# Another order for the branches' steps and their weights, and the norm rows loaded while the branches are merged

## The chip, the cores and the metric

The kernel runs as one program on one core of a Trainium2 chip. The time of a kernel is the device time of one execution in microseconds (us). Engines: PE is TensorE (matmuls and transposes; PEld its weight loads), DVE is VectorE, ACT is ScalarE, POOL is GpSimd, SP is SyncE, which here only issues transfers. Each engine works off its own instructions in the order in which the program holds them, and waits on semaphores of the others.

## The reference, cut to what matters

A block of two layers is followed by a second block of two layers, on a sequence of 512 tokens of width 1024. Each layer of the first block runs four attention branches of four heads, gates each with a silu, merges them and ends in a layer norm:

```
h = x @ w_in                         # split into the inputs of all branches
y_mla = causal softmax attention on rms-normed latents c_q, c_kv (w_qb, w_kvb), with rope
y_sb  = stick-breaking attention: a = exp(z + suffix sums of log_sigmoid(-z)), causal
y_fox = causal softmax attention, logits + (c_t - c_s), c = cumsum(log_sigmoid(fox_f + bias))
y_mem = softmax attention on keys and values made of mem (256 rows)
for n, y in enumerate((y_mla, y_sb, y_fox, y_mem)):
    merged += sigmoid(merge_r @ w_merge_up)[n] * ((y * silu(gate_z[n])) @ w_branch[n])
x = layer_norm(ALPHA * x + merged @ w_out, ln_g, ln_b)
```

Each layer of the second block runs four other branches of four heads (a dense, b a window with a sink, c a neighbourhood, d a difference of two softmaxes), gated with silu too, `x = x + mix @ w_out`, and the last row is normed. All is float32.

## The kernel before, in words

All tokens of a layer are on the chip at once. A product in float32 precision is made of three matmuls on split halves (`mm3`, L328 to L330): the two factors are split into a rounded high part (on ACT, L319) and the rest (on DVE, L322). A projection by one 128x1024 weight unit is so 24 matmuls of 128x512 (`proj`, from `proj_fm`). The halves of x stand in `zth`, `ztl`.

A layer of the first block is woven of generators, one for each branch, that yield after each step. `ORDER1` is a string of words that says which generator makes its next step: `first` (two memory queries and one stick query), `g` (a gate: one `proj` unit copied to `z`; after the gates of certain branches one more step runs their silus on ACT), `sb` (7 steps: keys, values, two heads, queries and keys, two heads), `mem` (5: keys and values, four heads), `fox` (8: row sums, queries and keys, values, two heads, queries and keys, two heads), `mla` (12: five latents, their norm, values and the rope queries, keys and queries, two heads, keys and queries, two heads), `misc`, and `f`, which takes the oldest ended pair of heads, divides it by its sums and multiplies it into its gate. `ORDER2` does the same for the second block (a, b, c, d, g, f, and w for a first part of the output product). `WEIGHTS1` and `WEIGHTS2` give the order in which the weight units come in, each by one transfer of 512 KB on SP and a split on ACT and DVE; `w_get` keeps three units ahead (`WP`).

The strings give the order of the program; a scheduler then places each instruction in its engine's own sequence, so that steps lie between each other. A head's chain is: scores on PE into one of three PSUM banks (`s`), a maximum on DVE (L525, L528), exp on ACT (L534), transposes on PE (`T`, L551), their split on ACT and DVE (`th`, `tl`), and the product with the values on PE (`O`, L557, L558). A stick head (`stick_head`) does four blocks: scores, then abs, exp and ln on ACT (L881 to L883) and max on DVE (L884), sums on PE (L894), exp on ACT (L896), the product on PE (`Os`, L900, L901). Silu and sigmoid need another function table on ACT than exp and ln; each change is an ACT_TABLE_LOAD.

After the heads the gated branches `z` are split (`split_z`), `merge` multiplies them by `w_branch` (`projwb`) and their merge gates (`projmu`), and `w_out` and `post` end the layer in four pieces of 128 tokens: product (`pso`), residual (L1127), layer norm (`ln_rows`), transposes back into `zth` and `ztl`. `end` loads the norm's rows `lng` and `lnb` (L1173), and `w_out` the residual rows (L1119), into a pool that is opened when the merge's pool is closed.

Of the kernel before, what the change touches and what calls it, by code (L numbers as in the profile page):

```python
# [18 lines left out]
S = 512  # L19
# [44 lines left out]


WEIGHTS1 = """
mq:0 mq:1 sb:0 gz:6 sb:256 sbv:0 sbv:1 sbv:2 gz:7 gz:2 gz:3 m:0 m:1 mk:0 mk:1 mv:0 mv:1 sb:128 sb:384 fox:0
fox:256 cq:0 cq:1 cq:2 gz:4 gz:5 ckv:0 ckv:1 foxv:0 foxv:1 gz:0 gz:1 fox:128 fox:384 kvb qr qb mr mu:0 wb:0
wb:1 mu:1 wb:2 wb:3 mu:2 wb:4 wb:5 mu:3 wb:6 wb:7 wo:0 wo:1 wo:2 wo:3 wo:4 wo:5 wo:6 wo:7
"""  # L70
WEIGHTS2 = """
qa:0 qa:1 ka qd:0 qd:1 kd qc:0 vd g2:6 g2:7 g2:0 g2:1 vab:0 vab:1 g2:2 g2:3 qb2:0 g2:4 qb2:1 kc:0 kb g2:5 vc:0
qc:1 kc:1 vc:1 we:0 we:1 wo2:0 wo2:1 wo2:2 wo2:3 wo2:4 wo2:5
"""

# [216 lines left out]

ORDER1 = "first g sb2 g misc sb g2 mem4 fox sb3 mem fox g mla f mla g3 mla2 fox mla f2 fox sb g f fox g fox mla fox mla fox mla g f mla f mla f mla2 f"
ORDER2 = "a d3 c d g2 d g2 d a d g f g2 a b a2 f g b c b a b2 g c f c g c d f2 c b f c b c f2 w2"
# [14 lines left out]
class Build:  # L311
# [275 lines left out]

    def new_o(self, r=None):
        return self.op.tile([128, S], F32, tag="o", name="o")

    def gate(self, key, at):

# [311 lines left out]
    def mla(self, l):  # L904
# [31 lines left out]
        qsc = self.kp.tile([128, 4, 2], F32, tag="qsc", name="qsc")  # L936
        nc.vector.tensor_scalar(qsc[:, :, 0], rs[:, :, 0], 96.0**-0.5, None, ALU.mult)
        nc.vector.tensor_scalar(qsc[:, :, 1], rs[:, :, 0], -(96.0**-0.5), None, ALU.mult)
        d = self.tmp("diag").rearrange("p (a b) -> p a b", b=128)
        nc.vector.tensor_copy(d, rs[:, :, 1:2].to_broadcast([128, 4, 128]))  # L940
        rep = self.pst.tile([128, S], F32, tag="T", name="rep")
        for tt in range(4):
            nc.tensor.transpose(rep[:, cols(tt)], d[:, tt], self.ident)
        for c in craw:
            h, lo = self.st("ckh"), self.st("ckl")
            nc.vector.tensor_tensor(c, c, rep, ALU.mult)
# [162 lines left out]
    def w_out(self, kind, l, lhs, post, last):  # L1109
        nc = self.nc  # L1110
        ks = range(len(lhs[0]))
        for k in ks:
            self.w_get((kind, l, k))
        woh, wol = self.wout
        for tt in range(4):
            c = cols(tt)
            y = self.bp.tile([128, DM], F32, tag="y", name="y", bufs=2)
            if kind == "wo":
                nc.sync.dma_start(y, self.resid[c])  # L1119
            fs = [cols(0, 512), cols(1, 512)]  # L1120
            if last and tt == 3:
                fs[1:] = [cols(2, 256), cols(3, 256)]
            for f in fs:
                ps = self.pss.tile([128, S], F32, tag="S", name="pso")[:, : f.stop - f.start]
                self.mm3(ps, [(lhs[0][k][:, c], lhs[1][k][:, c], woh[:, k, f], wol[:, k, f]) for k in ks])
                if kind == "wo":
                    nc.vector.scalar_tensor_tensor(y[:, f], y[:, f], ALPHA, ps, ALU.mult, ALU.add)  # L1127
                else:
                    nc.vector.tensor_tensor(y[:, f], self.early[tt][f.start // 512][:, f.start % 512 :][:, : f.stop - f.start], ps, ALU.add)
            post(tt, y, fs)  # L1130
# [25 lines left out]
    def ln_rows(self, y, g, b):  # L1156
        nc = self.nc
        st, mv, v = self.small(12, "bn"), self.small(2, "mv"), self.small(1, "var")
        for hf in range(2):
            nc.vector.bn_stats(st[:, cols(hf, 6)], y[:, cols(hf, 512)])  # L1160
        nc.vector.bn_aggr(mv, st.rearrange("p (a b) -> p a b", b=6))
        nc.vector.tensor_scalar(v, mv[:, 1:2], LN_EPS, None, ALU.add)
        for hf in range(2):
            f = cols(hf, 512)
            nc.vector.scalar_tensor_tensor(y[:, f], y[:, f], mv[:, 0:1], g[:, f], ALU.subtract, ALU.mult)
        rs = self.rsqrt(v)
        for hf in range(2):
            f = cols(hf, 512)
            nc.vector.scalar_tensor_tensor(y[:, f], y[:, f], rs, b[:, f], ALU.mult, ALU.add)

    def row(self, i, name):
        t = self.bp.tile([128, DM], F32, tag=name, name=name, bufs=1)
# [3 lines left out]
    def run(self):  # L1176
        nc, tc = self.nc, self.tc
        self.setup()
        for L in self.layers:
            l, kind = L % 2, "wo" if L < 2 else "wo2"  # L1180
            last = L == self.layers[-1]
            self.resid = self.ins["x"] if L == self.layers[0] else self.xs[L - 1]
            left = (self.layer1 if L < 2 else self.layer2)(l)
            nk = 8 if L < 2 else 6
            with tc.tile_pool(name=f"b{L}", bufs=1, side="right") as wop, left:
                self.wout = [wop.tile([128, nk, 1024], F32R, tag=f"wo{i}", name="wout") for i in range(2)]
                if L < 2:
                    left.close()
                    with tc.tile_pool(name=f"m{L}", bufs=3, side="left") as mp:
                        self.y = {n: self.split_z(n, mp) for n in MERGE}  # L1190
                        self.merge(l, mp)
                    lhs = [[t[:, k] for k in range(8)] for t in (self.zth, self.ztl)]
                else:
# [6 lines left out]
    def end(self, L, kind, lhs, last):  # L1200

        nc, l = self.nc, L % 2
        if L < 2:
            g, b = self.row(2 * l, "lng"), self.row(2 * l + 1, "lnb")
        gn = self.row(6 if L == 3 else 3 + L, "rmsg") if L == 3 or L in (1, 2) and not last else None

        def post(tt, y, fs):
            c = cols(tt)
            if L < 2:
                self.ln_rows(y, g, b)  # L1210
            if not last:
                nc.sync.dma_start(self.xs[L][c], y)
            if gn is not None:
# [260 lines left out]
```

## Time and profile before

| | us |
|---|---|
| median of 3 runs (1413.12 to 1415.84) | 1414.28 |
| the profiled execution's own time | 1410.68 |
| its span, from the first to the last instruction | 1408.9 |
| PE busy | 1350.6 |
| DVE busy | 1002.5 |
| ACT busy | 828.6 |

The span is that of the core's instructions; the execution's time has 1.8 us more around it. The page's busy time of PE counts matmuls that overlap each other, so 96% is the share of time in which PE had some matmul, not that of its peak. The first projections of the four layers start at 6, 415, 819 and 1112 us. In the rows, a wait is put down to the instruction that released it.

### The profile page before, as it was taken

Reading aid. Unit: us, or ns where it says so; the run is one execution under the profiler, and the core shown is the slowest. Engines: PE = TensorE matmul, PEld = TensorE weight load, DVE = VectorE, ACT = ScalarE, POOL = GpSimd, SP = SyncE. Lnnn points to the kernel's source line nnn. Section 1 sums busy time; section 2 is a strip of 40 time slices with the busy share of each in tenths; the row PEclk is TensorE's granted clock in tenths of the full one; section 3 lists DMA queues with packets and bytes.
Section 4 is the critical chain, followed back from the end, with each engine's and each line's share of the span. In section 5 each row is a group of like instructions: output and inputs, shape, how many; then the busy total and the mean of one; then the engine's idle time right before and its main releaser. Section 6 shows DMA issues by size and latency. Waiting matters only on the chain.

```text
span 1408.9 us, 19990 instructions
## 1 busy us (share of the span) xinstructions
PE 1350.6 (96%) x7096; PEld 1103.6 (78%) x7096; DVE 1002.5 (71%) x2077; ACT 828.6 (59%) x1672; POOL 4.3 (0%) x12
## 2 busy tenths in 40 slices
PE   8999998999999999998999999999999999999897
PEld 7887786777789777876777788877777888878776
DVE  5666545898773777257989775888787576877785
ACT  4585547765413775376856243775865446667663
POOL 0000000000000000000000000000000000000000
PEclk9999999899999999999999999999999999999999
DMA  7543323213625434222125536413535365215241
GB/s 231 166 128 92 90 77 80 61 52 103 232 105 127 142 90 130 75 74 72 48 90 171 182 109 178 122 61 82 143 93 155 117 174 155 62 55 152 66 135 73
DMA packets 61266, 160.31 MB, mean 114 GB/s; under 512 B 11056, under 2 KB 11696, under 8 KB 61168
## 3 DMA queue, kind: packets, MB, share of 16 engines
q1 hardware_dynamic: 61168, 159.05, 38.3%
q8 instruction: 56, 0.92, 0.3%
q14 instruction: 42, 0.34, 0.1%
HBM read 117.92 MB, written 8.91 MB: 90 GB/s over the span
## 4 chain that ended last, share of the span: by engine, by line
PE 75%; DVE 10%; ACT 8%; DMA 4%; issue 2%; SPq 0%; DVEq 0%; ACTq 0%
PE proj L328 11%; PE proj L329 11%; PE proj L330 10%; PE T L551 4%; PE pso L328 3%; PE pso L330 3%; PE pso L329 3%; PE O L557 3%; DMA raw<-in_w_dram 2%; PE O L558 2%; PE projwb L329 2%; PE projwb L328 2%; PE projwb L330 2%; PE projv L329 2%; PE projv L330 2%; PE projv L328 2%
## 5 line engine op out<-in xcount | busy, mean ns | idle before, releaser
L328 PE MATMUL proj<-zth,wh 128*128 128x512 f32 (+1 forms) x864 | 321.7, 373 | 8.3 <-ACT wh L319 5.6
L329 PE MATMUL proj<-ztl,wh 128*128 128x512 f32 (+1 forms) x864 | 322.4, 373 | 0.2
L330 PE MATMUL proj<-zth,wl 128*128 128x512 f32 (+1 forms) x864 | 321.0, 372 | 0.0
L322 DVE TENSOR_TENSOR wl<-raw,wh 128x1024 fp32r<-128x1024 f32 (+2 forms) x153 | 182.8, 1195 | 127.5 <-ACT wh L319 124.5
L319 ACT CAST wh<-raw 128x1024 fp32r<-128x1024 f32 (+2 forms) x153 | 157.5, 1029 | 149.0 <-PE proj L329 112.6
L328 PEld LDWEIGHTS proj<-zth,wh 128*128 128x128 f32 x864 | 164.0, 190 | 33.1 <-ACT wh L319 5.6
L330 PEld LDWEIGHTS proj<-zth,wl 128*128 128x128 f32 x864 | 164.0, 190 | 24.8 <-DVE wl L322 1.0
L329 PEld LDWEIGHTS proj<-ztl,wh 128*128 128x128 f32 x864 | 164.0, 190 | 24.1 <-DVE ztl L322 0.7
L322 DVE TENSOR_TENSOR tl<-T,th 128x512 fp32r<-128x512 f32 (+3 forms) x176 | 99.5, 576 | 36.7 <-ACT th L319 35.6
L319 ACT CAST th<-T 128x512 fp32r<-128x512 f32 (+3 forms) x176 | 85.1, 498 | 55.9 <-PE T L551 53.0
L551 PE MATMUL T<-ct,p 128*128 128x128 f32 x560 | 89.0, 279 | 5.2 <-ACT p L534 4.0
L528 DVE TENSOR_REDUCE nm<-s 128x1 f32<-128x512 f32 (+1 forms) x128 | 77.5, 614 | 14.8 <-PE s L1388 7.6
L551 PEld LDWEIGHTS T<-ct,p 128*128 128x128 f32 x560 | 67.8, 142 | 23.1 <-ACT p L534 7.0
L557 PE MATMUL O<-tl,V 128*128 128x512 f32 (+3 forms) x160 | 62.2, 390 | 8.3 <-DVE tl L322 7.4
L534 ACT ACTIVATE p<-s,nm 128x512 f32<-128x512 f32 (+1 forms) x96 | 59.1, 619 | 16.3 <-DVE nm L528 15.9
L558 PE MATMUL O<-th,V 128*128 128x512 f32 (+3 forms) x160 | 56.5, 355 | 0.0
L328 PE MATMUL pso<-wout,zth 128*128 128x512 f32 x128 | 51.1, 399 | 4.7 <-DVE y L1127 4.7
L329 PE MATMUL projv<-wl,zth 128*128 128x256 f32 (+1 forms) x192 | 54.9, 286 | 0.0
L328 PE MATMUL projv<-wh,zth 128*128 128x256 f32 (+1 forms) x192 | 54.6, 284 | 0.0
L330 PE MATMUL projv<-wh,ztl 128*128 128x256 f32 (+1 forms) x192 | 54.4, 283 | 0.0
L328 PE MATMUL projwb<-y,wh 128*128 128x512 f32 x128 | 51.5, 402 | 0.2
L330 PE MATMUL projwb<-y,wl 128*128 128x512 f32 x128 | 51.5, 403 | 0.0
(380 smaller groups left out, 2904.6 us busy)
## 6 DMA issues: line engine op xcount, KB each, us to landing
raw<-in_w_dram SPq DMA_DIRECT2D x173, 512.0 KB, 4.3
xs<-y SPq DMA_DIRECT2D x12, 512.0 KB
ks<-hs SPq DMA_DIRECT2D x32, 128.0 KB, 2.3
early<-xs SPq DMA_DIRECT2D x16, 256.0 KB, 3.8
bias<-in_bias_dram SPq DMA_DIRECT2D x8, 448.0 KB, 4.0
qs<-hs SPq DMA_DIRECT2D x24, 128.0 KB, 3.4
qs<-ls SPq DMA_DIRECT2D x24, 128.0 KB, 2.3
hs<-ls SPq DMA_DIRECT2D x24, 128.0 KB, 2.6
```

The lines of the kernel that those rows point to most:

```text
L319: self.nc.scalar.copy(h, src)
L322: self.nc.vector.tensor_tensor(l, src, h, ALU.subtract)
L328: self.nc.tensor.matmul(ps, ah, bh, start=i == 0, stop=False)
L329: self.nc.tensor.matmul(ps, ah, bl, start=False, stop=False)
L330: self.nc.tensor.matmul(ps, al, bh, start=False, stop=i == n - 1)
L528: nc.vector.tensor_reduce(nm, s, AX.X, ALU.max, negate=True)
L534: nc.scalar.activation(p[:, :w], src, AF.Exp, bias=nm, scale=sc, accum_out=sm)
L551: nc.tensor.transpose(T[:, cols(a)], P[i][:, c : c + 128], self.ident)
L557: nc.tensor.matmul(o, vsel(j), tl[:, :w], start=j == 0, stop=False, skip_group_check=True)
L558: nc.tensor.matmul(o, vsel(j), th[:, :w], start=False, stop=j == nk - 1, skip_group_check=True)
```

## The change

Four things are edited.

- The order of the steps, in `ORDER1` and `ORDER2`, and that of the weight units with it. The numbers of steps are the same. In the first block the latents (`mla`) begin before the last two stick heads, the last stick head comes ahead of the first forget-gate head instead of behind it, and the last gate unit (`gz:1`) comes behind the projections of the second forget-gate pair instead of ahead of them, with its silu behind that. In the second block steps of a, d and the gates change places.
- The norm rows and the residual rows of the first two pieces are loaded by `load_rows`, eight transfers of 256 KB into the eight buffers of the gates' pool `z`, each of which comes free when its gate has been split; the call stands between the split and the merge.
- The residual of pieces 0 and 1 is read from there (`rows`), and `ln_rows` takes the two halves of each norm row.
- In `mla` the copy `diag` falls away: four transposes read a broadcast of `rs` instead.

```diff
-ORDER1 = "first g sb2 g misc sb g2 mem4 fox sb3 mem fox g mla f mla g3 mla2 fox mla f2 fox sb g f fox g fox mla fox mla fox mla g f mla f mla f mla2 f"
+ORDER1 = "first sb g sb g misc sb g2 mem3 fox mem sb2 fox mem mla2 sb g2 mla g mla f fox mla f2 sb fox2 g2 fox g mla f fox mla g fox mla f2 mla f mla3 f"
...
+    def load_rows(self, l):
+        def load(src):
+            ts = [self.zp.tile([128, S], F32, tag="z", name="row") for _ in range(2)]
+            for hf, t in enumerate(ts):
+                self.nc.sync.dma_start(t, src(cols(hf, 512)))
+            return ts
+
+        self.resid_rows = {0: load(lambda f: self.resid[cols(0), f])}
+        self.lng, self.lnb = (load(lambda f: self.ins["rows"][2 * l + i, f].partition_broadcast(128)) for i in range(2))
+        self.resid_rows[1] = load(lambda f: self.resid[cols(1), f])
...
-        d = self.tmp("diag").rearrange("p (a b) -> p a b", b=128)
-        nc.vector.tensor_copy(d, rs[:, :, 1:2].to_broadcast([128, 4, 128]))
...
-            nc.tensor.transpose(rep[:, cols(tt)], d[:, tt], self.ident)
+            nc.tensor.transpose(rep[:, cols(tt)], rs[:, tt, 1:2].to_broadcast([128, 128]), self.ident)
...
+            rows = self.resid_rows.get(tt) or [y[:, f] for f in (cols(0, 512), cols(1, 512))]
-            if kind == "wo":
+            if kind == "wo" and tt not in self.resid_rows:
                 nc.sync.dma_start(y, self.resid[c])
...
-                    nc.vector.scalar_tensor_tensor(y[:, f], y[:, f], ALPHA, ps, ALU.mult, ALU.add)
+                    nc.vector.scalar_tensor_tensor(y[:, f], rows[f.start // 512], ALPHA, ps, ALU.mult, ALU.add)
...
                         self.y = {n: self.split_z(n, mp) for n in MERGE}
+                        self.load_rows(l)
                         self.merge(l, mp)
...
-            g, b = self.row(2 * l, "lng"), self.row(2 * l + 1, "lnb")
```

Three places show what the scheduler made of it. The first is ACT in layer 0 at the last pair of silus (`z`), before: `zt` and `at` belong to the last stick head, `p` to a forget-gate head.

```order
L601 ACTIVATE z_2260<-z_2260 128x512
L883 ACT_TABLE_LOAD
L883 ACTIVATE zt_2180<-zt_2180 128x256
L601 ACT_TABLE_LOAD
L601 ACTIVATE z_2366<-z_2366 128x512
L896 ACT_TABLE_LOAD
L896 ACTIVATE at_2193<-s_2176 128x256
L881 ACTIVATE zt_2205<-s_2201 128x384
L457 ACTIVATE hs_2430<-proj_2405 128x512
L882 ACTIVATE zt_2205<-zt_2205 128x384
```

One table load stands ahead of these rows and three behind them, up to the one of L604. The same pair after:

```order
L614 ACT_TABLE_LOAD
L614 ACTIVATE z_2330<-z_2330 128x512
L414 CAST V_2489<-projv_2491 128x4x64
L414 CAST V_2489<-projv_2508 128x4x64
L614 ACTIVATE z_2450<-z_2450 128x512
L414 CAST V_2490<-projv_2491 128x4x64
L414 CAST V_2490<-projv_2508 128x4x64
L617 ACT_TABLE_LOAD
```

Seven loads have become two, since nothing of a head lies between the silus: the stick head has ended before. It is the same in layer 1, and no other place has another number of loads.

The second is PE in layer 0 at the fourth forget-gate head, before: its last scores `s_2695`, the product `O_2585` of the head ahead of it, and its first transposes `T_2703`.

```order
L512 MATMUL s_2695<-ks_2482,qs_2434 128x512
L513 MATMUL s_2695<-kr_2478,qr_2435 128x512
L557 MATMUL O_2585<-tl_2602,V_1923 128x384
L558 MATMUL O_2585<-th_2601,V_1923 128x384
L551 MATMUL T_2616<-ct_79,p_2581 128x128
L557 MATMUL O_2585<-tl_2611,V_1923 128x256
L558 MATMUL O_2585<-th_2610,V_1923 128x256
L557 MATMUL O_2585<-tl_2619,V_1923 128x128
L558 MATMUL O_2585<-th_2618,V_1923 128x128
L551 MATMUL T_2703<-ct_79,p_2698 128x128
```

After, `s_2696` are that head's last scores, and `projn` and `s_2749` projections and scores of the next branch:

```order
L512 MATMUL s_2696<-ks_2446,qs_2398 128x512
L513 MATMUL s_2696<-kr_2442,qr_2399 128x512
L328 MATMUL projn_2942<-ckh_2055,wh_2407 128x512
L329 MATMUL projn_2942<-ckl_2056,wh_2407 128x512
L330 MATMUL projn_2942<-ckh_2055,wl_2408 128x512
L328 MATMUL projn_2942<-ckh_2060,wh_2407 128x512
L329 MATMUL projn_2942<-ckl_2061,wh_2407 128x512
L330 MATMUL projn_2942<-ckh_2060,wl_2408 128x512
L328 MATMUL s_2749<-mh_2638,mh_2660 128x128
L329 MATMUL s_2749<-ml_2639,mh_2660 128x128
L328 MATMUL projn_2961<-cqh_1568,wh_2483 128x512
L328 MATMUL s_2759<-mh_2638,mh_2660 128x256
```

Its first transposes come 13 matmuls later: 23 matmuls now stand between its last scores and its transposes (13 of 128x512 of `projn`, 10 of scores), where 7 short ones stood.

The third is SP in layer 0 at the merge, after, where `raw` are weight units (the first is `wb:3`, the second `mu:2`); before, the same two stood behind each other and nothing else came in.

```order
L597 DMA row_3207<-in_x_dram 128x512
L597 DMA row_3208<-in_x_dram 128x512
L597 DMA row_3211<-in_rows_dram 128x512
L597 DMA row_3212<-in_rows_dram 128x512
L376 DMA raw_3400<-in_w_dram 128x1024
L597 DMA row_3215<-in_rows_dram 128x512
L597 DMA row_3216<-in_rows_dram 128x512
L597 DMA row_3219<-in_x_dram 128x512
L597 DMA row_3220<-in_x_dram 128x512
L376 DMA raw_3406<-in_w_dram 128x1024
```

At the layer's end, before, the norm and residual rows came behind the weights of the next layer:

```order
L376 DMA raw_4234<-in_w_dram 128x1024
L1173 DMA lng_3805<-in_rows_dram 128x1024
L1173 DMA lnb_3807<-in_rows_dram 128x1024
L1119 DMA y_3845<-in_x_dram 128x1024
L1119 DMA y_3933<-in_x_dram 128x1024
```

Four transfers have left that place, two of the norm and two of the residual, and `mu:2` stands behind eight loads that wait for the gates' splits.

## Rows read from the trace of the kernel before

**Rows 1.** The page: span, and each engine's busy time (share) and instructions.
```profile
span 1408.9 us, 19990 instructions
PE 1350.6 (96%) x7096; PEld 1103.6 (78%) x7096; DVE 1002.5 (71%) x2077; ACT 828.6 (59%) x1672; POOL 4.3 (0%) x12
```

**Rows 2.** Waits of PE, whole span: total us, times, longest us.
```profile
PE O L557 <- DVE tl L322: 9.1, 11, 1.7
...
PE pso L328 <- DVE y L1127: 4.7, 2, 2.9
```

**Rows 3.** Windows: stretch, length, busy us by engine, clock, DMA; layers 0 and 1.
```profile
222.00:239.00 17.00, 13.28 (x75) 10.29 (x74) 10.70 (x25) 12.42 (x24) 0.00 (x0) 1.00 0.52 134
239.00:250.00 11.00, 9.64 (x33) 7.71 (x32) 7.53 (x24) 7.23 (x23) 0.00 (x0) 0.55 0.00 1
...
260.00:264.00 4.00, 3.67 (x13) 2.87 (x14) 3.07 (x7) 2.87 (x7) 0.00 (x0) 0.58 0.27 68
264.00:302.00 38.00, 37.12 (x204) 29.37 (x203) 35.32 (x97) 31.55 (x73) 0.00 (x0) 1.00 0.18 48
...
642.00:646.00 4.00, 3.24 (x10) 2.29 (x10) 2.73 (x5) 1.72 (x5) 0.00 (x0) 0.61 0.24 84
...
662.00:666.00 4.00, 3.10 (x12) 2.33 (x13) 3.29 (x8) 3.24 (x7) 0.00 (x0) 0.67 0.26 66
```

**Rows 4.** Waits of PE at 220 to 262 us; the last row at 625 to 665.
```profile
PE Os L900 <- DVE a L322: 2.7, 2, 1.8
PE T L551 <- ACT p L534: 2.0, 1, 2.0
PE s L894 <- DVE zt L884: 1.0, 1, 1.0
PE O L557 <- DVE tl L322: 0.7, 1, 0.7
PE T L551 <- DVE o L586: 0.5, 1, 0.5
...
PE projqr L328 <- DVE V L415: 0.6, 1, 0.6
```

**Rows 5.** Timeline of ACT at the silus of 214 us: start, us, line, operation.
```profile
213.80 0.44 ACT L882 ACTIVATE zt<-zt 128x256 f32<-128x256 f32 x1
214.26 1.28 ACT L601 ACT_TABLE_LOAD   x1
215.56 0.63 ACT L601 ACTIVATE z<-z 128x512 f32<-128x512 f32 x1
...
227.38 1.28 ACT L604 ACT_TABLE_LOAD   x1
```

**Rows 6.** Timelines at the ends of layers 0 and 1; in brackets idle time before.
```profile
374.35 0.42 SPq L1173 DMA_DIRECT2D lnb<-in_rows_dram  x1
374.83 1.21 SPq L1119 DMA_DIRECT2D y<-in_x_dram  x2
...
383.26 1.28 DVE L1127 SCALAR_TENSOR_TENSOR y<-y,pso 128x512 f32<-128x512 f32 x2 [7.46 <-DMA y<-in_x_dram]
384.01 0.50 PE L328 MATMUL pso<-wout,zth 128*128 128x512 f32 x1 [1.76 <-DVE y L1127]
...
788.01 0.50 PE L328 MATMUL pso<-wout,zth 128*128 128x512 f32 x1 [2.95 <-DVE y L1127]
```

**Rows 7.** Waits of PE at 150 to 158 us.
```profile
PE O L557 <- DVE tl L322: 0.9, 1, 0.9
PE proj L328 <- DVE cql L925: 0.8, 1, 0.8
```

**Rows 8.** The gates' splits at 280 to 312 us, SP at 308 to 313, one copy.
```profile
L322 DVE TENSOR_TENSOR y<-z,y x8: 673/682/685, 284.3 to 307.9; 128x512 fp32r<-128x512 f32 x8
...
312.19 0.33 SPq L376 DMA_DIRECT2D raw<-in_w_dram  x1
...
L940 DVE COPY diag<-rs_y x2: 419/420/421, 200.5 to 605.3; 128x512 f32<-128x512 f32 x2
```

**Rows 9.** Waits of PE at 1000 to 1100 us.
```profile
PE O L557 <- DVE tl L322: 2.9, 3, 1.7
PE Tv L440 <- ACT vc L1424: 0.8, 2, 0.5
```

More of the change, by code (lines that the diff above doesn't have):

```diff
@@ L66 @@
 WEIGHTS1 = """
-mq:0 mq:1 sb:0 gz:6 sb:256 sbv:0 sbv:1 sbv:2 gz:7 gz:2 gz:3 m:0 m:1 mk:0 mk:1 mv:0 mv:1 sb:128 sb:384 fox:0
-fox:256 cq:0 cq:1 cq:2 gz:4 gz:5 ckv:0 ckv:1 foxv:0 foxv:1 gz:0 gz:1 fox:128 fox:384 kvb qr qb mr mu:0 wb:0
+mq:0 mq:1 sb:0 sb:256 gz:6 sbv:0 sbv:1 sbv:2 gz:7 gz:2 gz:3 m:0 m:1 mk:0 mk:1 mv:0 mv:1 sb:128 sb:384 fox:0
+fox:256 cq:0 cq:1 cq:2 gz:4 ckv:0 gz:5 ckv:1 foxv:0 foxv:1 gz:0 fox:128 fox:384 gz:1 kvb qr qb mr mu:0 wb:0
 wb:1 mu:1 wb:2 wb:3 mu:2 wb:4 wb:5 mu:3 wb:6 wb:7 wo:0 wo:1 wo:2 wo:3 wo:4 wo:5 wo:6 wo:7
@@ L71 @@
 WEIGHTS2 = """
-qa:0 qa:1 ka qd:0 qd:1 kd qc:0 vd g2:6 g2:7 g2:0 g2:1 vab:0 vab:1 g2:2 g2:3 qb2:0 g2:4 qb2:1 kc:0 kb g2:5 vc:0
+qa:0 qa:1 ka qd:0 qd:1 kd qc:0 vd g2:6 g2:7 g2:0 g2:1 vab:0 vab:1 g2:2 g2:3 qb2:0 g2:4 kc:0 qb2:1 kb g2:5 vc:0
 qc:1 kc:1 vc:1 we:0 we:1 wo2:0 wo2:1 wo2:2 wo2:3 wo2:4 wo2:5
@@ L290, in cols @@
     return slice(n * i, n * i + n)
-ORDER1 = "first g sb2 g misc sb g2 mem4 fox sb3 mem fox g mla f mla g3 mla2 fox mla f2 fox sb g f fox g fox mla fox mla fox mla g f mla f mla f mla2 f"
-ORDER2 = "a d3 c d g2 d g2 d a d g f g2 a b a2 f g b c b a b2 g c f c g c d f2 c b f c b c f2 w2"
+ORDER1 = "first sb g sb g misc sb g2 mem3 fox mem sb2 fox mem mla2 sb g2 mla g mla f fox mla f2 sb fox2 g2 fox g mla f fox mla g fox mla f2 mla f mla3 f"
+ORDER2 = "a d3 c d2 g2 d g2 a g d g f a g b a g f a c b2 a b2 g c g f c d c2 f2 b c f b c f2 w2"
 GATES1, SILU1 = (3, 1, 2, 0), {1: (6, 7, 2, 3), 2: (4, 5), 0: (0, 1)}
@@ L1164, in ln_rows @@
             f = cols(hf, 512)
-            nc.vector.scalar_tensor_tensor(y[:, f], y[:, f], mv[:, 0:1], g[:, f], ALU.subtract, ALU.mult)
+            nc.vector.scalar_tensor_tensor(y[:, f], y[:, f], mv[:, 0:1], g[hf], ALU.subtract, ALU.mult)
         rs = self.rsqrt(v)
@@ L1168, in ln_rows @@
             f = cols(hf, 512)
-            nc.vector.scalar_tensor_tensor(y[:, f], y[:, f], rs, b[:, f], ALU.mult, ALU.add)
+            nc.vector.scalar_tensor_tensor(y[:, f], y[:, f], rs, b[hf], ALU.mult, ALU.add)
     def row(self, i, name):
@@ L1181, in run @@
             last = L == self.layers[-1]
+            self.resid_rows = {}
             self.resid = self.ins["x"] if L == self.layers[0] else self.xs[L - 1]
@@ L1202, in end @@
         nc, l = self.nc, L % 2
-        if L < 2:
-            g, b = self.row(2 * l, "lng"), self.row(2 * l + 1, "lnb")
         gn = self.row(6 if L == 3 else 3 + L, "rmsg") if L == 3 or L in (1, 2) and not last else None
@@ L1209, in post @@
             if L < 2:
-                self.ln_rows(y, g, b)
+                self.ln_rows(y, self.lng, self.lnb)
             if not last:
```

## The prediction

> **What bounds the kernel now.** I read the page first, then the waits of PE over the whole span, then windows around the stretches that these pointed to, and timelines inside them. The page shows PE with a matmul in flight for 1350.6 of 1408.9 us [rows 1]. The change neither adds nor removes a product, so all that it can win is time in which PE stands still or runs at its low clock. That is 1408.9 - 1350.6 = 58 us of idle time, and some more hidden in matmuls that are stretched.
>
> The reader is to see that the idle time is not spread evenly. The windows [rows 3] show layer 0 at 222 to 239 us: PE busy 13.28 of 17 us, DVE 10.70, ACT 12.42, the clock full. Right behind it, at 239 to 250, the granted clock reads 0.55, so for most of it PE ran at 1.2 instead of 2.4 GHz. A second dip (0.58) lies at 260 to 264. Layer 1 has the same two places, with dips at 642 to 646 (0.61) and 662 to 666 (0.67). From 264 to 302 us PE is busy 37.12 of 38 and DVE 35.32 (93%): there the heads are close to a second limit, DVE.
>
> What PE waits for at 220 to 262 us [rows 4]: twice the last stick head's output, 2.7 us; its sums, 1.0; a forget-gate head's output, 0.7; an output's sum, 0.5; and for one exp before a head's transposes, 2.0. Layer 1 has the same list without the 0.5 and with 0.6 instead of 0.2 for the rope queries.
>
> Why the stick head is late stands in the timeline of ACT [rows 5]. Between 214.26 and the end of the load at 227.38 (228.66) lie seven table loads of 1.28 us, 9.0 of 14.4 us. The two silus are put between the stick head's exp and ln, and each side needs its own table.
>
> The third place is the end of a layer. The residual's sum waits for its transfer, 7.46 us of idle DVE in layer 0, and PE waits 1.76 us for it; in layer 1 2.95 us [rows 6], together the 4.7 of the whole list [rows 2].
>
> **The change part by part.** All sums go against the profiled execution, 1410.68 us with 1.8 us around the span; the median of the three runs is 3.60 us above it, and I add that at the end.
>
> *Table loads and the last stick head.* The order shows seven loads become two in each of the first two layers: 5 x 1.28 = 6.4 us of ACT gone per layer, at the place where the waits of rows 4 begin. These loads themselves are not on PE's path, so I price the waits that follow: 2.7 + 1.0 + 0.7 + 0.5 = 4.9 us in layer 0, 2.7 + 1.0 + 0.7 = 4.4 in layer 1, 9.3 in all. The stick head itself isn't gone; it runs earlier, beside `gz:0` and the first forget-gate projection. Its four blocks wait in the same way there, without the loads. Bounds: 0 (the waits move with it) to 9.3. I take 8.0, nearer the upper end, because two or three of its score blocks already lie ready there and projections stand between its sums and its outputs.
>
> The row shows 1.28 us for a load and 0.04 us of pause on its two sides [rows 5]. The Trainium skill (ScalarE: Activation LUTs, section What ACT_TABLE_LOAD costs) adds a drain of about 1.38 us to each switch, 2.66 in all; by that five switches would be 13.3 us per layer, more than the whole wait, and I would take 9.3 for 8.0, which makes the time 1.3 us shorter. The trace shows no such pause here, so I stay with 8.0.
>
> *The low clock behind it.* Time lost is the missing share of the clock times PE's busy time: (1 - 0.55) x 9.64 = 4.3 us at 239 to 250 and (1 - 0.61) x 3.24 = 1.3 at 642 to 646 [rows 3]. Both stretches follow the stick head's waits directly, and with the clock full before them. If those go, so do these: 5.6. Bounds: 0 to 5.6; I take all of it, as it hangs on the item above.
>
> *The fourth forget-gate head.* PE waited 2.0 us for its exp in each layer [rows 4], and the dips at 260 and 662 follow, (1 - 0.58) x 3.67 = 1.5 and (1 - 0.67) x 3.10 = 1.0. The order now puts 13 projection matmuls and 10 of scores between this head's scores and its transposes. But the same six late heads then have less left beside them, and at 264 to 302 DVE had 7% of its time free: what is not waited for here is partly waited for later. So 4.0 + 2.5 = 6.5 at most, and below nothing too, to -4 if the waits of a late head are repeated once more in each layer. I take half of the upper end, 3.2.
>
> *Residual and norm rows.* The waits of 1.76 and 2.95 us end when the residual is in place before the merge's last product: 4.7 us. Nothing else was late at that spot, as the product's banks are freed by this one sum. The norm's rows are needed later than the residual and come earlier as well. Bounds 3.5 to 4.7; I take 4.7. The added wait: eight transfers on SP wait for the gates' splits, the last of which on DVE starts at 307.9 [rows 8], and `mu:2` is queued behind them. Before, `mu:2` was issued at 312.19 because its buffer came free then, not because of SP; so the wait is covered by 3.5 us (307.9 + 0.7 to 312.2). If the heads ended later than that, `mu:2` would shift by as much, and the merge with it once its own lead is used up.
>
> *Early part of layers 0 and 1.* At 150 to 158 us PE waits 0.9 and 0.8 us where two heads and a latent meet [rows 7], and the same in layer 1: 3.4 in all. The order now spreads these heads over more projections, but the second wait, for the latent's half, is still met, with the same chain behind an output. Bounds -2 to 3.4; I take 1.5.
>
> *`diag`.* One copy of 0.42 us per layer on DVE is gone [rows 8]; nobody waited for it. Transposes that read a broadcast are not in this trace; they are as many and as large as those they replace, so I bound them by the copy itself, -0.4 to 0.4 per layer, and take zero.
>
> *Second block.* The heads keep their places up to half a head, loads and silus their number. The waits of layer 2 at the end (2.9, 0.8 and smaller ones [rows 9]) lie where no projection is left, and that is so after too. Bounds -4 to 4 for both layers; I take 0.
>
> Sum: 8.0 + 5.6 + 3.2 + 4.7 + 1.5 = 23.0 us. 1410.68 - 23.0 = 1387.7, and 1414.28 - 23.0 = 1391.3 as a median.
>
> **The rivals.**
> *The late heads are held by DVE.* For it: 93% at 264 to 302, and less projection work beside the six late heads. Against: at 222 to 260 DVE is far from full. Then the fourth head's term becomes its lower end (-4), and half of the stick head's waits and of the clock come back (6.8 left of 13.6): 6.8 - 4 + 4.7 + 1.5 = 9.0, so 1405.3.
>
> *Nearly all idle time in these places goes.* For it: waits on DVE and ACT while both have room. Then 9.3 + 8.1 (all four dips) + 4.0 + 4.7 + 3.4 + 4 (second block) = 33.5, so 1380.8. Against: heads never ran without waits in any layer of this trace.
>
> *Slower: the clock falls among the late heads.* Mechanism: with the projections spent earlier, PE stands still often between the late heads, as at 222 to 239 (22% idle), and the low clock that followed it there follows each such stretch. One costs up to 4.3 us. The late heads fill about 240 to 302, room for five such stretches. With five in each layer instead of today's 8.1 us in all: 43 - 8.1 = 35 lost, 8.0 + 4.7 + 1.5 won, so 21 us slower, 1435; it decides from about three and a half per layer, where it cancels the gains. At four per layer, 34.4 - 8.1 - 14.2 = 12 slower, 1426.4, the value I give it. Against: at 264 to 302 the clock read 1.00 with the same kind of heads. The Trainium skill (TensorE: Matmul & The Clock Gate, section A second HAM failure mode: psum-queue depth-cycling) tells of a kernel whose clock swings because PE idles briefly and often between groups of matmuls; by that rule this rival would deserve more than I give it, and rows 3 at 264 to 302 speak against it.
>
> *It does not do what it says.* The stick head waits as long in its new place, the low clock with it, the fourth head gains nothing, and only the rows' 4.7 us come, against losses of 2 early and of 2 in the second block: 0.7, so 1413.6.
>
> **How the numbers follow.** The forecast gets 0.50, DVE holding the heads 0.18, nearly all 0.12, the clock 0.12, nothing 0.08. Of this kernel a measurement can tell 0.2% (2.8 us) from no change. Faster are the first three: 0.80. Within 0.2%: 0.08. Slower: 0.12. The range leaves out the clock rival and the outer parts of the others. The forecast's own range is 1384 to 1399 (the stick and clock items together between 8 and 15, the fourth head -2 to 6, early and second block plus or minus 3); with the rivals it reaches from 1379 to 1413, which holds the first three cases and half of the last.
>
> **What would show it.** Right: in layers 0 and 1 two table loads at the last silus; no waits of the stick output near `kvb`; the clock full through the late heads; no wait of 1.7 to 3 us at the start of `pso`'s third product; the fourth forget-gate head's transposes without a wait of 2 us. Wrong: DVE over 95% through the late heads with PE under 95% (the first rival), stretches with the clock near 0.5 there (the clock), the waits on `Os` at the new place at the same length (the last), or `mu:2` landing late and a wait of `projmu` in the merge. A gain in layers 2 and 3 of over 4 us each way would mean that I underrated the second string.

## The result and the profile after

The changed kernel takes 1374.26 us (median of 4 runs, 1373.08 to 1377.81), the kernel before on the same chip 1413.73 (1413.12 to 1415.84). The ratio is 0.9728, with a 95% interval of 0.9705 to 0.9751: 35 to 42 us less. Forecast were 1391.3 us and a range from 1379: the direction and the main mechanism hold, but the gain is larger than the range allowed.

The page answers to [rows 1]: the same 7096 matmuls, PE busy 12 us less, ten table loads fewer on ACT. The mean granted clock of the two profiled executions, 0.992 and 0.995, accounts for some 4 of these 12 us (0.003 of 1350.6, an estimate); what makes up the rest is not shown.

```profile
span 1372.2 us, 20002 instructions
PE 1338.4 (98%) x7096; PEld 1099.4 (80%) x7096; DVE 1002.0 (73%) x2075; ACT 816.4 (59%) x1662; POOL 4.3 (0%) x12
```

The first product of each layer and the last of all give the layers' lengths in the two profiled executions:

| us | layer 0 | layer 1 | layer 2 | layer 3 |
|---|---|---|---|---|
| before | 409.0 | 403.9 | 293.6 | 290.1 |
| after | 394.2 | 392.1 | 288.9 | 285.0 |
| difference | -14.9 | -11.7 | -4.7 | -5.1 |

So the first block wins 26.6 us, where the whole forecast was 23.0, and the second block 9.8, where it was 0.

The waits of PE after, whole span (total us, times, longest us), answer to [rows 2, 4, 7]. The last row is one of before.

```profile
PE s L512 <- DVE sums L525: 3.9, 2, 2.0
PE projqr L328 <- DVE V L415: 2.7, 2, 1.4
...
PE O L557 <- DVE tl L322: 1.1, 4, 0.4
...
PE Os L913 <- DVE a L322: 0.7, 4, 0.2
...
PE projqr L328 <- DVE V L415: 0.7, 2, 0.6
```

The stick outputs, 2.7 us in each of two layers before, are down to 0.7 in all; the heads' outputs went from 9.1 to 1.1; the residual is gone from the list. One row is new, the score bank (`s` for `sums`), once each in layers 2 and 3; and the wait of the rope queries for values (`projqr` for `V`) in layers 0 and 1 has grown from 0.7 to 2.7.

Windows after (length, then busy time of PE, PEld, DVE, ACT, POOL, the granted clock, DMA share, GB/s) answer to [rows 3]:

```profile
232.00:240.00 8.00, 6.58 (x37) 5.51 (x37) 3.95 (x12) 7.78 (x16) 0.00 (x0) 1.00 0.24 89
240.00:262.00 22.00, 20.57 (x110) 15.71 (x109) 20.86 (x58) 17.93 (x45) 0.00 (x0) 1.00 0.43 119
262.00:300.00 38.00, 37.09 (x191) 28.47 (x192) 36.23 (x86) 28.59 (x63) 0.00 (x0) 1.00 0.26 79
...
618.00:640.00 22.00, 19.93 (x99) 16.23 (x98) 11.34 (x29) 13.59 (x28) 0.00 (x0) 0.92 0.43 117
...
1003.00:1010.00 7.00, 5.06 (x27) 4.44 (x26) 5.80 (x16) 5.62 (x16) 0.00 (x0) 0.79 0.38 103
```

The clock stays full through the late heads of layer 0, with DVE at 95% there, and dips a little in layer 1 (0.92). A new low place lies in layer 2. ACT at the last silus, answering to [rows 5], has two loads, without a head's work between the silus:

```profile
231.95 1.28 ACT L614 ACT_TABLE_LOAD   x1
233.24 0.63 ACT L614 ACTIVATE z<-z 128x512 f32<-128x512 f32 x1
...
234.30 0.64 ACT L614 ACTIVATE z<-z 128x512 f32<-128x512 f32 x1
234.83 0.65 ACT L414 CAST V<-projv 128x256 fp32r<-128x256 f32 x2
235.49 1.28 ACT L617 ACT_TABLE_LOAD   x1
```

The rows' transfers on SP stand in the merge's beginning, and the next weights behind them (answering to [rows 6, 8]):

```profile
279.56 2.50 SPq L597 DMA_DIRECT2D row<-in_x_dram  x2
...
289.56 4.94 SPq L597 DMA_DIRECT2D row<-in_x_dram  x2
297.68 3.85 SPq L376 DMA_DIRECT2D raw<-in_w_dram  x2
```

### The profile page after: what moved, and what is told of

It reads as the page before. It is cut to its first block, busy times and chain, and to the rows that moved or that the text cites. A ratio compares the mean times of both kernels' runs of the same rounds, so it can differ in the third digit from the quotient of the medians.

```text
span 1372.2 us, 20002 instructions
## 1 busy us (share of the span) xinstructions
PE 1338.4 (98%) x7096; PEld 1099.4 (80%) x7096; DVE 1002.0 (73%) x2075; ACT 816.4 (59%) x1662; POOL 4.3 (0%) x12
## 4 chain that ended last, share of the span: by engine, by line
PE 80%; DVE 8%; ACT 7%; DMA 2%; issue 2%; SPq 0%; DVEq 0%; ACTq 0%
PE proj L328 11%; PE proj L329 11%; PE proj L330 11%; PE T L551 4%; PE pso L330 3%; PE pso L329 3%; PE pso L328 3%; PE O L557 2%; PE O L558 2%; PE projwb L329 2%; PE projwb L328 2%; PE projwb L330 2%; PE s L512 2%; DMA raw<-in_w_dram 2%; PE s L513 2%
## 5 line engine op out<-in xcount | busy, mean ns | idle before, releaser
L1107 ACT ACTIVATE sg<-projmu 128x512 f32<-128x512 f32 x64 | 38.1, 598 | 22.7 <-DVE sg L1114 11.6
```

What stands on the lines that cost most here:

```text
L1107: a = nc.scalar.activation(sg, ps, AF.Sigmoid)
```

## The experiments

"Theory A" is mine in each. Every run lies against the kernel before on its own chip, whose medians there were 1407.7 to 1414.4 us. "First" and "second" are the lengths of the two blocks in the profiled execution, from first product to first product (the last ends with the last product); before they are 812.9 and 583.7.

| kernel | median us | gain us by the ratio (95%) | first | second |
|---|---|---|---|---|
| e1 first block's order | 1394.62 | 18.5 (12.6 to 24.4) | 795.5 | 583.7 |
| e2 second block's order | 1401.88 | 10.4 (6.2 to 14.7) | 813.8 | 572.7 |
| e3 rows | 1408.94 | 4.0 (1.0 to 6.9) | 810.1 | 585.9 |
| e4 diag | 1412.07 | 1.6 (-1.6 to 4.8) | 809.1 | 583.9 |
| e5 second order, last third | 1422.06 | -8.2 (-11.2 to -5.1) | 811.4 | 592.9 |
| e6 second order, first two thirds | 1398.49 | 15.0 (9.5 to 20.6) | 815.1 | 572.3 |
| e7 before, two silus left out | 1398.30 | 15.7 (10.0 to 21.3) | 800.6 | 583.8 |
| e8 before, stick head earlier | 1418.94 | -5.8 (-9.0 to -2.7) | 820.9 | 584.1 |
| e9 latent earlier | 1406.60 | 5.4 (2.8 to 8.0) | 815.8 | 577.7 |
| e10 gates spread | 1407.50 | 4.8 (1.4 to 8.2) | 811.6 | 577.5 |
| e11 changed, old second block | 1384.54 | 25.5 (22.3 to 28.9) | 785.7 | 585.1 |
| e12 changed, old last third | 1373.07 | 36.8 (33.9 to 39.8) | 785.2 | 572.8 |
| e13 changed, tail filled | 1373.90 | 41.3 (37.6 to 44.8) | 786.9 | 573.6 |
| e14 changed, finish later | 1379.81 | 34.8 (31.3 to 38.5) | 787.0 | 580.0 |
| e15 changed again | 1373.74 | 39.5 (35.8 to 43.3) | 784.8 | 573.5 |
| e16 first order, no diag | 1392.82 | 15.5 (13.1 to 17.7) | 795.4 | 583.6 |
| e17 first order + rows | 1388.81 | 19.7 (17.0 to 22.4) | 790.3 | 585.0 |

The block with an unchanged order shows how much one execution differs from another: the second reads 583.6 to 585.9 in nine kernels that have it as before, the first 809.1 to 815.8 in eight that have its order as before (e3 and e4 among them, with their own edits). So 10 us in the second block are plain, 3 us in the first are not.

**One part at a time.** e1 takes only the two tables of the first block, e2 only those of the second, e3 only `load_rows` and what reads its tiles, e4 only the lines on `diag`, all as the change has them:

```
-ORDER1 = "first g sb2 g misc sb g2 mem4 fox sb3 mem fox g mla f mla g3 mla2 fox mla f2 fox sb g f fox g fox mla fox mla fox mla g f mla f mla f mla2 f"
+ORDER1 = "first sb g sb g misc sb g2 mem3 fox mem sb2 fox mem mla2 sb g2 mla g mla f fox mla f2 sb fox2 g2 fox g mla f fox mla g fox mla f2 mla f mla3 f"
-ORDER2 = "a d3 c d g2 d g2 d a d g f g2 a b a2 f g b c b a b2 g c f c g c d f2 c b f c b c f2 w2"
+ORDER2 = "a d3 c d2 g2 d g2 a g d g f a g b a g f a c b2 a b2 g c g f c d c2 f2 b c f b c f2 w2"
```

> The kernel before with only the first block's new order (the table of steps and the table of weights of layers 0 and 1). Theory A (the order of the first block acts by itself, in the stretch of the last heads: head waits, table loads, the low clock behind them and the last head's wait go; the two traces differ there by 11.8 us in layer 0 and 8.4 in layer 1): about 22 us less, 18 to 24. Rival B (the early part and the last heads gain only together with the free norm rows of the merge, since the table loads and the ring transfers meet): less than 15 us. Rival C (most of the gain is a drift between two profiled executions): under 10 us.

> The kernel before with only the second block's new order (table of steps and table of weights of layers 2 and 3). The prediction put this part at 0 with bounds of 4 us either way; the two traces differ by 4.7 and 5.1 us in these layers. Theory A (the order of layers 2 and 3 does it): 9 to 10 us less. Rival B (what comes earlier in layers 2 and 3 is left over from the first block, a transfer or a buffer that is free sooner): under 3 us less, and the rest appears in the run with only the first block's order.

> The kernel before with only the residual and norm rows loaded into separate tiles in the merge. Prediction's term: 4.7 us less (1.76 in layer 0, 2.95 in layer 1), bounds 3.5 to 4.7; the two traces differ by 1.5 and 3.0 there. Theory A: 4 to 4.7 us less, and no wait of the residual's product for VectorE's addition of more than 1 us. Rival B (the transfers of 2 MB at the start of the merge hold up weights on the same queue): under 2 us less, and a new TensorE wait for a weight in the merge.

> The kernel before without the four diagonal copies ahead of the replicating transposes (the transposes read the column broadcast). Prediction's term: 0, since the 0.42 us copy is VectorE's and TensorE has other work. Theory A: within 0.2 % (2.8 us) of before, by the trace 0 to 0.8 us less. Rival B (the broadcast operand makes the transposes slower or they begin later): 1 us or more slower.

By the ratio e1 came out inside its range, at its lower edge (the traces say 17.4 us, the medians 16.4), e2 near the 9 to 10 that were written down, with 11.0 in the second block by the traces: theory A in both. e3 agrees with 4.0, and its residual wait is gone. e4 can't be told from nothing; even so the scheduler's sequence in it is another one, with six table loads at the last silus of layers 0 and 1 instead of seven. The four gains add up to 34.5, the whole is 38.5 (35.2 to 41.7); e11, the changed kernel with `ORDER2` and `WEIGHTS2` of before, takes the second block out of it:

> The changed kernel with the second block's old order and weights table: first block's order, rows and diag together. Theory A (the parts add up, the second block's 11 us by the traces come off the changed kernel's gain): 26 to 29 us less than before. Rival B (the second block's gain is partly lost to the first block's): over 32 us less. By the prediction's sum this kernel is the whole forecast, 23 us less.

25.5 us by the ratio, just under theory A's range, 26.9 by the medians and 27.2 by the traces, inside it: theory A. It is the forecast's sum of 23.0 and a little more, and its second block reads 585.1 against 573.9 in the changed kernel.

**Are the table loads the cause?** e7 changes neither string; the two gates of the last branch are copied instead of passed through silu (`AF.Copy if at in (0, 1) and self.wl1 else AF.Silu`, with `wl1` true in layers 0 and 1), so its output lacks those silus.

> The kernel before, in which two of the eight gate tiles of layers 0 and 1 (those of the last branch) are copied instead of passed through silu, so that no table load stands among the late stick heads; what is computed leaves those two silus out. Theory A (the table loads cause the late head waits, and these the low clock behind them): up to 15 us less, from 4.9 + 4.3 in layer 0 and 4.4 + 1.3 in layer 1, at least 8. Rival B (the place of the heads is the cause: a stick head's exponentials and a forget-gate head's stand in one queue, tables or not): under 4 us less, head waits still over 1 us each.

Theory A: 15.7 us by the ratio, 12.3 in the first block by the traces (the whole order, e1: 17.4), with one load of 1.28 us left there. Its waits of PE at 210 to 262 us, and its clock where the kernel before had 0.55 [rows 3]:

```profile
PE projqr L328 <- DVE V L415: 1.3, 1, 1.3
PE s L512 <- DVE nm L525: 0.9, 2, 0.7
PE projn L328 <- DVE ml L973: 0.8, 1, 0.8
PE T L551 <- ACT p L534: 0.2, 1, 0.2
...
239.00:250.00 11.00, 9.16 (x44) 6.53 (x43) 9.22 (x25) 7.47 (x19) 0.00 (x0) 1.00 0.36 104
```

The stick head's steps stand in the string where they stood, and no wait for it is over 0.2 us: rival B, that the heads' place in the string is the cause, is out. Two things go with the loads. The scheduler weaves another sequence without them (the stick head's last product starts at 228.5 us, before at 238.3). And the fourth forget-gate head's wait for its exp, 2.0 us before, is down to 0.2 as well, though no step was moved to give it more work. e8 moves the stick head's step and leaves the gates:

```
-mla f2 fox sb g f fox g fox mla
+mla f2 sb fox g f fox g fox mla
```

> The kernel before with one step moved in layers 0 and 1: the last stick head's step ahead of a forget-gate head's. The gates and all else stay in their places. Theory A (the late stick heads stand too close to the late gates' silus; with one head earlier, fewer table loads lie in its chain): 3 to 10 us less. Rival B (the silus of the last gates decide, wherever the heads stand): within 3 us of before, seven table loads between the last heads as in before.

Both theories missed: it is 6 us slower. The scheduler put two loads more between the heads in each layer, nine for seven, and ACT is full (21.76 of 22 us). The low clock isn't the reason: the mean granted clock of its ten executions is 0.992, that of the kernel before on the same chip 0.988. The waits moved to other instructions of the same chain:

```profile
213.00:235.00 22.00, 18.20 (x86) 13.15 (x84) 10.71 (x32) 21.76 (x37) 0.00 (x0) 1.00 0.11 30
...
PE s L894 <- DVE zt L884: 2.2, 2, 1.2
PE projqr L328 <- DVE V L415: 1.8, 1, 1.8
```

So an earlier head alone wins nothing; e7 and e8 together point to the silus standing together, outside any head, as what wins in the changed kernel.

**Where the second block's gain comes from.** e5 and e6 split the string of `ORDER2` behind `b2 g`; e6 has `WEIGHTS2` as well.

> The kernel before with only the last third of the second block's step order changed (from the point where latents and gates are left to the merge weights). Theory A (the gain of the second block comes from the last projections of values standing between the pieces of a window head, and a latent head coming half a head sooner; the traces differ there by about 3 and 3.6 us per layer against 4.5 lost to a new wait on a score bank): 4 to 8 us less in all, with the bank wait of 2 us in each of layers 2 and 3. Rival B (the head of the order, with its gates spread and the weight loaded sooner, makes room for it): under 2 us less, or slower.

> The kernel before with only the first two thirds of the second block's step order and its weights table changed. Theory A of the last run: 0 to 2.5 us less (the 0.9 us per layer near the middle of the layer), the waits of 1.7 us on the window head's transposes and those behind them still there. Rival B: 6 us less or more.

Here my theory fell in both. The first two thirds bring all of the second block's gain (572.3 us, as with the whole order), the last third alone loses 8. PE's rows in e5 show why: the old wait stays, and a second one comes, for the square that the difference head's statistics need, with the low clock behind it.

```profile
PE statd L1270 <- ACT sqd L1401: 2.5, 1, 2.5
PE O L557 <- DVE tl L322: 1.7, 1, 1.7
...
1038.00:1043.00 5.00, 3.21 (x13) 2.88 (x14) 2.17 (x7) 4.02 (x12) 0.00 (x0) 0.58 0.09 20
```

What the first two thirds do stands in PE's timeline at the second of the four window heads of layer 2 (start, us, operation, idle before it in brackets). The kernel before has one projection left between two pieces of the head's output:

```profile
1010.07 0.34 PE L558 MATMUL O<-th,V 128*128 128x384 f32 x1
1010.25 0.39 PE L330 MATMUL proj<-zth,wl 128*128 128x512 f32 x1
1012.34 0.39 PE L557 MATMUL O<-tl,V 128*128 128x256 f32 x1 [1.71 <-DVE tl L322]
```

e6 has two scores and three projections there, and no wait:

```profile
1009.27 0.35 PE L558 MATMUL O<-th,V 128*128 128x384 f32 x1
1009.46 0.28 PE L512 MATMUL s<-ks,qs 128*128 128x256 f32 x1
1009.58 0.28 PE L513 MATMUL s<-ks,qs 128*128 128x256 f32 x1
1009.70 0.40 PE L330 MATMUL proj<-zth,wl 128*128 128x512 f32 x1
1009.93 0.39 PE L328 MATMUL proj<-zth,wh 128*128 128x512 f32 x1
1010.16 0.39 PE L329 MATMUL proj<-ztl,wh 128*128 128x512 f32 x1
1010.39 0.28 PE L557 MATMUL O<-tl,V 128*128 128x256 f32 x1
```

The number of projections is the same in both kernels; what differs is how many have been used up by then. Two more runs take the two shifts in these two thirds apart. e9 has only `c b2` for `b c b` (and `kc:0` ahead of `qb2:1`), e10 only the gates between the heads:

```
-a d3 c d g2 d g2 d a d g f g2 a b a2 f g b c b a b2 g
+a d3 c d2 g2 d g2 a g d g f a g b a g f a b c b a b2 g
```

> The kernel before with one thing of the second block's new first two thirds alone: the key latent's step `c` stands ahead of two window heads (c b2) instead of between them (b c b), its weight one place earlier. In the run with the whole of the new first two thirds the waits on the window head's output at the end of layers 2 and 3 (1.7 us each, with 0.5 on the values behind) are gone. Theory A (the latent's place does it, since value and query projections are then left beside the last window head): 5 us less or more, those waits gone. Rival B (the gates' places among the dense heads do it): under 2 us less, the waits of 1.7 us still there.

> The kernel before with the other thing of the second block's new first two thirds alone: the gates stand singly among the dense and difference heads, the latent's step and its weight where they were. Theory A of the last run: under 3 us less (only the 0.9 us near the middle of the layer). Rival B: 5 us less or more, waits of 1.7 us gone. If both runs win 5 us, either shift is enough to leave projections beside the last window head.

Each shortens the second block by 6 us (577.7 and 577.5), and neither theory is alone right: either shift leaves projections beside that head, and its long wait is gone in both. What stays at 1000 to 1060 us (first row e9, second e10; 2.9 us in three waits before [rows 9]) are two waits of the third window head, 0.86 and 0.31 us at 1044 us in e9, as long as in the kernel before:

```profile
PE O L557 <- DVE tl L322: 1.2, 2, 0.9
```

```profile
PE O L557 <- DVE tl L322: 1.3, 2, 1.0
```

In e6, which has both shifts, these are gone too: no wait for `tl` of over 0.2 us is left from 1000 us on.

**Does the new last third cost anything beside them?** e12 gives the changed kernel the old one back:

```
-c g f c d c2 f2 b c f b c f2 w2
+c f c g c d f2 c b f c b c f2 w2
```

> The changed kernel with the last third of the second block's step order as before, the first two thirds new. Theory A (alone, the new last third lost 8 us, and beside the new first two thirds it gains about what it loses: 4.5 us lost to the wait on a score bank with the clock behind it, 3.6 and less gained further on): 37 to 43 us less than before, within 3 us of the changed kernel or faster. Rival B (the new last third needs the new first two thirds and gains there): 33 us less or fewer.

36.8 us is just under theory A's range, the median 1373.07 is that of the changed kernel: the two last thirds are worth the same there. What the new one loses is the wait on a score bank. Only score products stand ahead of it, and it starts when DVE has made the `sums` from an earlier one's scores:

```profile
1003.10 0.28 PE L513 MATMUL s<-ks,qs 128*128 128x256 f32 x1
1005.33 0.44 PE L512 MATMUL s<-ks,qs 128*128 128x384 f32 x1 [1.94 <-DVE sums L525]
```

Two runs ask whether that can be had without the loss, a third measures the changed kernel beside them:

```
-c g f c d c2 f2 b c f b c f2 w2
+c g f c2 d c f2 b c f b c f2 w2     (e13)
+c g f c d c2 b f2 c f b c f2 w2     (e14)
```

> The changed kernel with the last third of the second block's order as c g f c2 d c f2 b c f b c f2 w2: the last difference head comes behind the second pair's query latent, so that 13 projections of vc:1 stand ahead of its statistics, where the changed kernel has seven score products. Theory A (for want of projections there PE waits 2 us on a score bank, and the low clock follows): both go, and the 3.6 us that the new last third wins further on stay; 4 to 9 us less than the changed kernel. Rival B (what is gained there is lost at the end of the layer, where the projections are now missing): within 2 us of the changed kernel, as with the old last third.

> The changed kernel with the two finishing steps behind the window head instead of ahead of it (c2 b f2 for c2 f2 b) in the second block's last third. The score products ahead of the statistics stay. Theory A of the run before: the wait of 2 us on a score bank stays, time within 2 us of the changed kernel. Rival C (the finishing work on VectorE ahead of the window head's sums makes the wait): the wait goes, 4 us less or more.

> The changed kernel unaltered, beside the two runs before on the same chip: 1374 us, 37 to 41 less than before. Both theories expect the same here; it is the measure for the other two.

In e13 the bank's wait and the low clock are gone, but the time is that of the changed kernel beside it (1373.90 and 1373.74): rival B. A wait for the values' transposes takes the place; that it comes because their projection now stands earlier is argued from the order, not shown by a run of its own. The first row is e13 at 985 to 1060 us. The other two are e14, where the bank's wait stays, as theory A had it (rival C is out), but which is 6 us slower, as theory A had not: the clock behind the wait falls lower, and the first part of the output product (`pse`) waits 2.9 us in all, where the changed kernel has no such wait.

```profile
PE Tv L440 <- ACT vc L1436: 1.4, 1, 1.4
```

```profile
PE pse L328 <- DVE early L1261: 2.9, 2, 1.5
...
1005.00:1015.00 10.00, 8.50 (x33) 7.35 (x34) 5.91 (x21) 6.13 (x19) 0.00 (x0) 0.66 0.54 136
```

No version beat the changed kernel by more than the runs can tell.

**Why rows and diag bring 9.8 us beside the new order.** From e1 to e11 the first block goes from 795.5 to 785.7. e16 is e1 without `diag`, e17 is e1 with the rows.

> The kernel before with the first block's new order and without the diagonal copies; rows loaded as before. Theory A (without the copy VectorE's work in the late part of layers 0 and 1 falls into another sequence, and the waits on the latents' low halves, 1.4 and 1.8 us, with the low clock behind, go): first block about 791 us by the trace, 3 to 6 us less than the new order alone, the residual's waits of 1.8 and 3.4 still there. Rival B (those waits have nothing to do with diag): within 2 us of the new order alone, 795.5.

> The kernel before with the first block's new order and the rows loaded in the merge; the diagonal copies stay. Theory A of the run before: the residual's waits go, 5 to 6 us less than the new order alone (first block about 790), the waits on the latents' low halves stay. Rival B (rows bring all of the 9.8): first block about 786 us, as in the changed kernel.

e17 takes the residual's waits away (5.2 us in e1) and wins 5.2: theory A. In e16 the waits for the latents' low halves (`ml`) went from 1.4 and 1.8 us to 0.3 in each layer, as theory A said, but the block's time stayed (795.4): rival B in time. Two things make up for it. A wait of the rope queries for values came in their place, 1.3 and 1.4 us. And in layer 0 the clock fell behind the residual's wait, where in e1 it did not. First e16's wait, then the clock in e1 and in e16:

```profile
PE projqr L328 <- DVE V L415: 1.3, 1, 1.3
...
370.00:375.00 5.00, 3.19 (x15) 2.29 (x14) 2.53 (x5) 0.00 (x0) 0.00 (x0) 1.00 0.68 277
...
370.00:375.00 5.00, 3.08 (x9) 2.25 (x9) 3.60 (x7) 0.00 (x0) 0.00 (x0) 0.77 0.39 158
```

The second is a matter of the single execution: of the eleven traces that have this wait in layer 0, the clock falls right behind it in two (e7 and e16). Over four executions each, e16 has the same mean granted clock as e1 (0.994), and its median, on another chip, is 1.8 us lower.

From e17 to e11, which differ by the copy alone, the first block goes from 790.3 to 785.7, but the trace of e17 has two stretches at the low clock there (at 250 and 642 us) and that of e11 none. So what leaving out the copy is worth beside the new order, somewhere from 0 to 5 us, these runs can't tell closer. What they do show is that more than the 0.42 us of the copy changes: without it the scheduler writes another sequence on PE and ACT in layers 0 and 1, and the table loads at the last silus are two in each layer (e16, e11), where the new order alone has three (e1, e17). Of the seven loads that became two, the order took four and the missing copy one.

## Why the prediction was right or wrong

*Stick head, low clock and fourth forget-gate head: right in size, but not separate.* The prediction gave the loads 8.0 + 5.6 us and put the fourth head's wait beside them, 3.2 us, won by work between its scores and its transposes. e7, which takes away the loads alone, ends that wait too, and both dips near it; whether by the earlier exp or by the products that the scheduler then puts ahead of the transposes is not shown. So its 15.7 us (10.0 to 21.3; 12.3 by the traces) stand against 8.0 + 5.6 + 3.2 = 16.8. That the low clock hangs on the waits is borne out over the executions: e7's four have a mean granted clock of 0.995, the nineteen of the kernel before on the same chip 0.988. By what the clock costs in the kernel before (last section), that is 6 to 7 of the 15.7 us, an estimate. But the dip priced at 4.3 us is not there in every execution of the same order.

The prediction set a rule of the Trainium skill (ScalarE: Activation LUTs, What ACT_TABLE_LOAD costs) against the rows, 2.66 us for a switch with its drain. Here again the row says 1.28: the silu starts 0.01 us behind its load, and the load of 235.49 0.01 us behind the work ahead of it.

*Late heads as a whole, and early part: right in kind.* Lining up the two traces, the late heads give 11.8 us in layer 0 and 8.4 in layer 1, 20.2 against the same 16.8. The early part gave 1.5 in layer 0 and nothing in layer 1, against 1.5.

*Residual and norm rows: right.* 4.3 us of 4.7 by the lined-up traces, 4.0 in e3, 5.2 beside the new order (e1 waited 1.8 and 3.4 us). The 5.2 is not the new order's doing: with the first block's old order the two waits add up to 4.6 in e5 and 5.3 in e2. The cover for `mu:2` held: no wait of over 0.2 us at 300 to 330 us.

*`diag`: right alone (e4), too small in company.* The term counted the copy's time and held the rest of the sequence fixed. The scheduler wrote another sequence, with one table load less in each of two layers; its worth is not known to better than a few us.

*Second block: the step that failed.* "The waits of layer 2 at the end (2.9, 0.8 and smaller ones [rows 9]) lie where no projection is left, and that is so after too. Bounds -4 to 4 for both layers; I take 0." It measured 9.8 us in the changed kernel and 11.4 in e6. The step that failed is the premise that no projection is left there either way. The kernel before had its last one between the pieces of that head, e6 has three there and more behind, and the wait of 1.71 us went. The premise was checked against the end of the layer and not against the string's middle: shifts of half a head there decide how many projections are left at 1010 us. The prediction named the sign that came true (over 4 us in each of layers 2 and 3), but it weighed the work beside the heads for the first block alone and did not carry this to the second.

*From the profile to the median.* The forecast took its 23.0 us from the median, 3.6 above the profiled execution. The changed kernel's profile lies 0.3 under its median. So the miss of 17.0 us is 9.8 for the second block, 3.6 for the first (26.6 - 23.0), 3.3 for this step (3.6 - 0.3) and 0.3 outside the layers. The step is largely clock: the profiled execution before was granted 0.992, the 89 others of that kernel 0.989 in the mean, so what was priced from its rows was less low clock than most executions have.

*The rivals.* Late heads held by DVE: DVE is at 95% from 240 to 300 us, and PE still at 96%, so no. The clock among the late heads: full in layer 0, no. Its price has a wrong sum: at 4.3 us each, the gains cancel from 2.6 stretches per layer (22.3 / 8.6), not from three and a half. The forecast's own range too is added up wrongly at its slow end: 8 - 2 + 4.7 - 1.5 (3 off the 1.5 of the early part and the second block) = 9.2 gives 1405, not 1399. Neither changes the outcome. The rival's rule from the Trainium skill (TensorE: Matmul & The Clock Gate, A second HAM failure mode: psum-queue depth-cycling) tells of a clock that swings while PE idles between groups of matmuls; no run here shows such swings. What the traces show is single: at the score bank of layer 2 one wait of 1.94 us and one stretch at 0.79 behind it. Nearly all idle time goes (1380.8 us, 0.12) was nearest, and still too slow by 6.5.

## What to carry to other kernels

Where a string of steps sets which filler work stands beside which chain, a wait late in a layer may be owed to a shift much earlier, so count the filler that is left at each wait instead of asking whether a head moved. Put work that needs another ACT table where no chain on the other table is open; moving the chain without the table's users can make it worse. Where a scheduler writes the sequence, an edit that looks free, such as one copy less, can change the whole of it: compare the sequences before you price the edit alone. Price a wait of PE with the clock behind it as a range, and look at the granted clock of every execution before you read a few us from one trace.

## What the runs showed of the hardware

The same instructions were granted different clocks. e2, e5, e6, e9 and e10 have the same 4383 matmuls in the same order as the kernel before, up to 876 us. In e5 the waits ahead are as long and PE is busy 13.21 of 17 us at 222 to 239 (13.28 before), and yet the clock behind it was full, while it read 0.53 to 0.55 in the kernel before and in the other four:

```profile
239.00:250.00 11.00, 8.91 (x46) 7.06 (x47) 8.28 (x27) 8.71 (x26) 0.00 (x0) 1.00 0.00 1
```

Lined up product by product against the kernel before, that one place is worth 2.7 us in e5. (e4 read 1.00 there too, but in another sequence with a load less.)

Over whole executions the time of one kernel goes with the clock that it is granted. The 89 executions of the kernel before that ran beside the experiments were granted 0.981 to 0.996 of the clock in the mean. Those at 0.981 took 1420.9 us, those at 0.995 1407.4, and a straight line through all 89 gives 9.7 us for 0.01. The changed kernel, granted 0.993 to 0.998, ran from 1371.85 to 1379.39. A dip read from one profile is therefore a chance with a price, not a fixed cost.
